# A two-layer hybrid backbone: the order of the feed-forward products, where the modulation is computed, and the last norm's sums

## The chip, the cores and the metric

The kernel runs on one core of a Trainium2 chip. The metric is the device time of one execution in microseconds. Five engines work side by side, each through its own queue in order: TensorE (PE) for matrix products, VectorE (DVE), ScalarE (ACT), GpSimd (POOL), and SyncE (SP), from which this kernel issues its DMAs. An instruction at the head of a queue that waits holds up everything behind it on that engine.

## The reference

Two layers over 1024 latent and 256 context tokens of width 1024, in fp32. Layer 0 mixes tokens by latent attention and windowed attention side by side, layer 1 by differential attention. What the change touches is the modulation, the feed-forward part and the norms:

```python
def layer_norm(x, g, b):
    mu = jnp.mean(xf, -1, keepdims=True)
    var = jnp.mean(jnp.square(xf - mu), -1, keepdims=True)
    return ((xf - mu) * lax.rsqrt(var + LN_EPS) * g + b).astype(x.dtype)

def conv_ffn(h, w_gate, w_up, conv_w, conv_b, w_down):
    g = h @ w_gate
    gp = jnp.pad(g, ((0, 0), (1, 1), (0, 0)))
    g = gp[:, :-2] * conv_w[0] + gp[:, 1:-1] * conv_w[1] + gp[:, 2:] * conv_w[2] + conv_b
    return (jax.nn.silu(g) * (h @ w_up)) @ w_down

def modulation(cond, w_mod, b_mod):
    return jnp.split(jax.nn.silu(cond) @ w_mod + b_mod, 6, axis=-1)

for i in range(DEPTH):
    sh1_l, sc1_l, gt1_l, sh2_l, sc2_l, gt2_l = modulation(c, w_mod[i], b_mod[i])
    ...
    xl = layer_norm(ALPHA * xl + gt1_l * o_l, ln1_g[i], ln1_b[i])
    h_l = xl * (1.0 + sc2_l) + sh2_l
    f_l = conv_ffn(h_l, ffn_w_gate[i], ffn_w_up[i], ffn_conv_w[i], ffn_conv_b[i], ffn_w_down[i])
    xl = layer_norm(ALPHA * xl + gt2_l * f_l, ln2_g[i], ln2_b[i])
```

The hidden width is 2816. Context tokens take the same path in layer 0 with the second conditioning vector `c_ctx`; in layer 1 only the first two of the six modulation vectors are needed for them.

## The kernel before

Activations lie with features on the 128 partitions and tokens along the free dimension. Tokens come in three tiles: 0 and 1 (512 latent tokens each) and 2 (256 context tokens). Every large product is done in a split form: an operand is written as a high part (`hi`, a copy on ACT) and a remainder (`lo`, a subtraction, on DVE or on POOL), and three matmuls stand for one product (`mm`, line 90). A 128 by 512 block of weights is split by `split`; its subtraction is line 87, the copy line 84.

**Seven products for eight.** In the feed-forward part both the up half (gate and up weights at once) and the down half treat their operands as two by two blocks, and use seven products P1 to P7 in place of eight, with sums and differences of blocks formed on DVE. `UP` and `DOWN` give the order of the seven. There are 22 blocks `f` of 128 hidden features. In the up half (`run_up`) one product is 12 matmuls of 512 columns. A first pass computes P1 and P2 for blocks 0 to 11 and writes the results to DRAM (`pre_d`), because these need token tile 0 alone, while the norm of tile 1 is still running. The second pass then does the other five products of blocks 0 to 11 (`EARLY` = 12), one after another, and after that all seven products of blocks 12 to 21. After its last product a block is finished (`finish`: convolution along tokens, silu, product with the up half; lines 1395 to 1399), and stored to DRAM as hidden block `f` two products into the next block. Beside this, `down_sums` forms sums of the down weights for hidden blocks `j` and `j + 11` and writes them to DRAM; it is called in blocks 0 to 10.

In the down half (`run_down`) each of P1 to P7 runs over 11 steps `j`; a step is 12 matmuls into four PSUM banks. Its hidden operand comes from `hidden_operand` (lines 1304 to 1324): P5 writes `b12 - b11` to a temporary tile (three buffers), P6 and P4 change hidden blocks in place. The results of a product are added to the residual by instructions that wait in a list, `late`, and are issued one per group of three matmuls in the next product. When P4 is done, token tile 0 is complete and its norm begins; when P3 is done, tile 1.

**Order of the work.** `advance` prepares operands ahead: six steps in the up half, three in the down half, and issues weight loads two further. Which subtractions go to POOL is written in `prepare`: up P2, P7, P4; down P5, P6, P4. A tile framework places instructions into the engine queues by order of issue and a model of when they are ready, so an instruction of a later step can be placed earlier where its operands and buffers allow it.

**Norms** are generators (`norm`, line 330) that sit in the list `behind`; `tick` advances the first one after every third matmul, and `settle` runs them to the end. A norm adds the eight feature blocks on DVE (line 356), takes their mean over partitions by a product with a constant matrix (line 362), subtracts it (line 351, or 349 on POOL), squares on ACT, adds the squares on DVE (line 373), sums them over partitions by small products (line 380), takes the inverse root, spreads it over partitions by one more product (line 287) and multiplies (line 351). Before each of its PE steps it lets `lag` = 3 ticks pass.

**Modulation of layer 1** (`mod_vectors`, line 163) is advanced beside the second pass of layer 0's up half, 72 advances over its length. For each of twelve halves of 512 values it loads eight 128 by 512 blocks of `w_mod` (two buffers, `opt`), multiplies each by the conditioning value of its partition and accumulates on DVE (lines 185, 187), for shift and scale (chunks 0 and 1) once for each of the two conditioning vectors; then it sums over partitions by four small products for each vector (line 197). The generator is emptied (`drain`) after the up half.

## Time and profile before

| | us |
|---|---|
| median of three runs | 3517.93 |
| lowest and highest | 3513.55, 3519.29 |
| profiled execution, own time | 3515.21 |
| its span | 3513.4 |
| PE / DVE / ACT / POOL busy | 3205.5 / 2650.5 / 1674.3 / 1097.7 |
| layer 0: first pass of the up half | 904.8 to 992.6 |
| second pass: five-product blocks, seven-product blocks | 992.6 to 1234.7, 1234.7 to 1435.1 |
| down half, context part | 1435.1 to 1686.3, 1686.3 to 1907.7 |
| layer 1: first pass | 2790.7 to 2869.3 |
| second pass: five-product blocks, seven-product blocks | 2869.3 to 3053.0, 3053.0 to 3249.0 |
| down half, tail after the last matmul of it | 3249.0 to 3480.2, 3480.2 to 3513.4 |

The span is the time from the first to the last instruction of one profiled execution. Lines such as L87 are lines of the kernel before. A busy PE counts overlapping matmuls, so the number of matmuls in a stretch tells more than its busy time. In a group of instructions, `out<-in` are the program's names of tiles, buffer numbers left out; behind the bar stand the busy time, the mean of one in ns, and the engine's idle time before them with what ended it. The granted clock of PE is 1.00 at full speed.

### The profile page before, as it was taken

The numbers are of one execution on the slowest core, as the hardware profiler recorded it, in microseconds if no ns is written. First come the engines' busy times: TensorE is split into PE (matmuls) and PEld (weight loads), VectorE is DVE, ScalarE is ACT, GpSimd is POOL, SyncE is SP. The second block draws the span as 40 slices with busy tenths as digits, with TensorE's granted clock in tenths as the row PEclk, the third lists the DMA queues.
The fourth block names the chain that finished last, engine by engine and source line by source line (L and its number), as shares of the span: only waits on it lengthen the run. The fifth ranks groups of instructions, "written<-read, shape, count | busy, mean of one in ns | idle before, by whom it ended". The sixth has DMA issues, their size and how long they took to land. (4 is left out here: it accounts for less than half of the span.)

```text
span 3513.4 us, 48532 instructions
## 1 busy us (share of the span) xinstructions
PE 3205.5 (91%) x16772; PEld 2632.9 (75%) x16772; DVE 2650.5 (75%) x4518; ACT 1674.3 (48%) x3161; POOL 1097.7 (31%) x848
## 2 busy tenths in 40 slices
PE   8998999999887899899799999998899999999996
PEld 4466778888666688678698887887778777788775
DVE  3137878875889989677888467778898789976677
ACT  3125778862532233334565345556677443333433
POOL 4245333421311121042543234344522222221132
PEclk9999999999888899999899999999999999999998
DMA  7666233222487744724465665547654468623622
GB/s 227 196 206 195 84 83 85 74 81 83 171 265 240 249 147 146 265 81 129 156 186 156 197 170 157 146 140 210 174 173 142 157 203 271 218 90 109 230 87 87
DMA packets 288007, 568.11 MB, mean 162 GB/s; under 512 B 24785, under 2 KB 111249, under 8 KB 285713
## 3 DMA queue, kind: packets, MB, share of 16 engines
q1 hardware_dynamic: 287760, 565.01, 51.2%
q8 instruction: 132, 2.16, 0.3%
q14 instruction: 115, 0.93, 0.1%
HBM read 419.35 MB, written 145.56 MB: 161 GB/s over the span
## 5 line engine op out<-in xcount | busy, mean ns | idle before, releaser
L87 POOL TENSOR_TENSOR al<-raw,ah 128x512 fp32r<-128x512 f32 x196 | 296.9, 1516 | 665.6 <-ACT ah L84 652.2
L84 ACT ACTIVATE ah<-raw 128x512 fp32r<-128x512 f32 x418 | 260.5, 630 | 434.3 <-PE f L90 294.8
L90 PE MATMUL s<-k,q 128*128 128x512 f32 (+2 forms) x1152 | 307.7, 389 | 15.8 <-ACT sxc L1877 6.8
L87 DVE TENSOR_TENSOR ptl<-tp,pth 128x512 fp32r<-128x512 f32 x412 | 279.6, 684 | 42.2 <-ACT pth L546 37.2
L546 ACT ACTIVATE pth<-tp 128x512 fp32r<-128x512 f32 x412 | 242.3, 595 | 104.9 <-PE tp L542 97.3
L84 ACT ACTIVATE ah<-sum 128x512 fp32r<-128x512 f32 x198 | 122.0, 629 | 342.9 <-DVE sum L1257 172.6
L542 PE MATMUL tp<-ident,p 128*128 128x128 f32 x1648 | 257.6, 276 | 20.7 <-DVE ptl L87 10.2
L90 PE MATMUL f<-al,ah 128*128 128x512 f32 x616 | 245.5, 398 | 10.5 <-DVE al L87 10.3
L90 PE MATMUL f<-ah,al 128*128 128x512 f32 x616 | 243.3, 395 | 7.5 <-POOL al L87 7.5
L90 PE MATMUL f<-ah,ah 128*128 128x512 f32 x616 | 241.3, 395 | 3.0 <-ACT ah L84 3.0
L542 PEld LDWEIGHTS tp<-ident,p 128*128 128x128 f32 x1648 | 197.6, 142 | 52.6 <-DVE ptl L87 10.1
L90 PE MATMUL o<-pth,v 128*128 128x256 f32 x976 | 232.7, 300 | 4.6 <-ACT pth L546 4.5
L87 DVE TENSOR_TENSOR al<-raw,ah 128x512 fp32r<-128x512 f32 x222 | 173.7, 795 | 77.9 <-ACT ah L84 77.8
L90 PEld LDWEIGHTS s<-k,q 128*128 128x128 f32 (+1 forms) x1152 | 189.9, 193 | 45.7 <-ACT p L1890 10.8
L87 POOL TENSOR_TENSOR al<-sum,ah 128x512 fp32r<-128x512 f32 x44 | 67.8, 1541 | 426.0 <-ACT ah L84 384.3
L90 PE MATMUL o<-ptl,v 128*128 128x256 f32 x656 | 185.8, 295 | 16.3 <-DVE ptl L87 15.6
L90 PEld LDWEIGHTS o<-pth,v 128*128 128x128 f32 x976 | 171.2, 192 | 24.2 <-ACT pth L546 7.9
L1887 DVE TENSOR_REDUCE stat<-s 128x1 f32<-128x1024 f32 x128 | 155.6, 1216 | 39.5 <-PE s L90 39.3
L1890 ACT ACTIVATE p<-s,stat 128x1024 f32<-128x1024 f32 x128 | 142.7, 1115 | 82.9 <-DVE stat L1888 67.6
L90 PE MATMUL f<-T,ah 128*128 128x512 f32 x528 | 168.7, 401 | 1.2 <-ACT ah L84 1.2
L90 PE MATMUL f<-b0h,ah 128*128 128x512 f32 x352 | 143.8, 409 | 14.4 <-ACT ah L84 8.8
L87 POOL TENSOR_TENSOR wl<-wraw,wh 128x1024 fp32r<-128x1024 f32 x36 | 91.2, 2533 | 202.7 <-ACT wh L84 200.8
(450 smaller groups left out, 9714.2 us busy)
## 6 DMA issues: line engine op xcount, KB each, us to landing
raw<-w_gate SPq DMA_DIRECT2D x90, 512.0 KB, 4.1
raw<-w_up SPq DMA_DIRECT2D x66, 512.0 KB, 4.3
raw<-w_down SPq DMA_DIRECT2D x66, 512.0 KB, 4.9
wm<-w_mod SPq DMA_DIRECT2D x96, 256.0 KB, 4.2
opt<-w_mod SPq DMA_DIRECT2D x96, 256.0 KB, 3.0
sd<-affy SPq DMA_DIRECT2D x88, 256.0 KB, 4.4
hid<-acc SPq DMA_DIRECT2D x44, 512.0 KB, 3.3
raw<-sd SPq DMA_DIRECT2D x88, 256.0 KB, 2.6
```

The source lines that it names most:

```text
L84: return self.nc.scalar.activation(out, src, AF.Copy)
L87: (eng or self.nc.gpsimd).tensor_tensor(out, src, hi.bitcast(F32), op=ALU.subtract)
L90: self.nc.tensor.matmul(out, lhsT, rhs, start=start, stop=stop)
L542: nc.tensor.transpose(ps[:, n * P : (n + 1) * P], pt[:, kc : kc + P], N.ident[:, :])
L546: nc.scalar.activation(h[:, : n * P], ps[:, : n * P], AF.Copy)
L1887: nc.vector.tensor_reduce(st[:, 2, b, m : m + 1], s[:, :], axis=AX.X, op=ALU.max)
L1890: nc.scalar.activation(p[:, :SEQ], s[:, :], AF.Exp, bias=mx, scale=scale, accum_out=sums[:, b, m, 0:1])
```

## The change

- The second pass of the up half takes blocks in the order 0, 1, 12, 2, 13, 3, ..., 21, 11, so that after two blocks of five products a block of seven and one of five alternate. `rank` is a block's place in this order. `down_sums` is called in every block of odd rank. The loads of hidden blocks for the down half, which were issued as the last block released its operands, start for P1 and P2 in block 21 and for the others in block 11.
- In the second pass P3's subtraction goes to POOL too.
- Chunks 0 and 1 of layer 1's modulation are computed in layer 0's up half by `mod_products`: for each loaded block, four fp32 products on PE with two columns, both conditioning vectors at once, accumulated in PSUM. Forty advances take the place of 72. Chunks 2, 3 and 4 are computed as before on DVE, in layer 0's down half (three advances in four steps, emptied after P4), chunk 5 in layer 1's up half.
- The down half runs P1, P2, P6, P7, P4, P5, P3. P5's operand is formed in place from what P6 left. POOL's subtractions are those of P6, P4, P5 and P3.
- `lag` is 6.
- The last norm (layer 1, tile 1; `alone`) adds the eight blocks by eight products with the constant matrix, adds the squares by small products in PSUM block by block, and lets POOL do two of the eight last multiplies.
- Before the up half the first weights are prepared ahead of the rest of the context tile's norm.

```diff
-        self.lag = 3
+        self.lag = 6
...
+    def mod_products(self, l, chunks, wpool, ppool, ptag):
...
+        for which, half in chunks:
+            ps = self.t(ppool, [P, 512], tag=ptag)
+            for k in range(KT):
+                w = ws.pop(0)
+                for j in range(4):
+                    nc.tensor.matmul(ps[:, 2 * j : 2 * j + 2], w[:, j * P : (j + 1) * P], self.siluc[:, k, 0:2],
+                                     start=k + j == 0, stop=k + j == KT + 2)
+                if todo:
+                    fetch()
+                if k % 2:
+                    yield
+            at = slice(8 * which + 4 * half, 8 * which + 4 * half + 4)
+            b = self.vecs[:, V_BMOD + 48 * l : V_BMOD + 48 * l + 48][:, at]
+            o = self.modv[l][:, at, :]
+            nc.vector.tensor_tensor(o, ps[:, :8].rearrange("p (j c) -> p j c", c=2), b.unsqueeze(2).broadcast_to([P, 4, 2]), op=ALU.add)
+            nc.vector.tensor_scalar(self.sc1[l][:, at, :], o, 1.0, None, op0=ALU.add)
+            yield
...
+        if alone:
+            mean = psum()
+            for i, k in enumerate((4, 5, 6, 7, 0, 1, 2, 3)):
+                nc.tensor.matmul(mean[:, :w], self.mean[:, :], x[k], start=i == 0, stop=i == KT - 1)
...
+                for b in range(nb if alone else 0):
+                    nc.tensor.matmul(st[:, b : b + 1], sq[k - 1][:, b * P : (b + 1) * P], self.mean[:, 0:1],
+                                     start=k == 1 and b == 0, stop=k == KT and b == nb - 1)
...
+        c = copy(bc) if alone else None
         for k in range(KT + 2):
             if k < KT:
-                each(k, bc, None, ALU.mult)
+                each(k, bc, c, ALU.mult)
...
-    DOWN = ("P1", "P2", "P5", "P6", "P7", "P4", "P3")
+    DOWN = ("P1", "P2", "P6", "P7", "P4", "P5", "P3")
...
-        early = [(f, p) for f in range(self.EARLY) for p in self.UP if p not in ("P1", "P2")]
-        rest = [(f, p) for f in range(self.EARLY, NF) for p in self.UP]
+        early, late = range(self.EARLY), range(self.EARLY, NF)
+        blocks = [*early[: -len(late)], *itertools.chain(*zip(late, early[-len(late) :]))]
+        rest = [(f, p) for f in blocks for p in self.UP if f in late or p not in ("P1", "P2")]
+        self.rank = {f: i for i, f in enumerate(blocks)}
...
-            a = self.split(self.raws.pop(n), None if p in ("P5", "P6", "P4") else self.N.nc.vector)
+            a = self.split(self.raws.pop(n), None if p in ("P6", "P4", "P5", "P3") else self.N.nc.vector)
...
-        self.parts[n] = self.split(src, None if p in ("P2", "P7", "P4") and n >= self.n_first else self.N.nc.vector)
+        self.parts[n] = self.split(src, None if p in ("P2", "P7", "P4", "P3") and n >= self.n_first else self.N.nc.vector)
...
-        if p == "P5":
-            return self.add(b12, b11, ALU.subtract)
...
-        put(b21, b21, b11, op=ALU.subtract)
-        return b21
+        if p == "P4":
+            put(b21, b21, b11, op=ALU.subtract)
+            return b21
+        put(b12, b22, b11, op=ALU.subtract)
+        return b12
...
-        for t in (0, 2) if l == 0 else (0,):
-            N.settle(t)
+        N.settle(0)
         N.op.update({p: [y[:, 4 * i : 4 * i + 4, :] for y in N.h[0]] for i, p in enumerate(("P1", "P2"))})
+        self.advance(0)
+        N.settle(2)
...
+            while gone < 40 * (n - self.n_first) // span:
+                next(mods, None)
+                gone += 1
+            if p == "P6" and at % 2:
+                self.down_sums(at // 2)
+            if p == "P7" and at:
+                store(self.blocks[at - 1])
+            if f == end or p in ("P1", "P2") and f == NF - 1:
                 self.leave(p)
...
-    def run_down(self, ready):
+    def run_down(self, ready, mods):
...
+            if n % 4:
+                next(mods, None)
             if j == final and p in ("P4", "P3"):
                 while late:
                     late.popleft()()
+                drain(mods)
                 ready(0 if p == "P4" else 1)
...
+    if l == 0:
+        mods = N.mod_products(1, halves((0, 1)), N.ls, N.qq, "f")
+        more = N.mod_vectors(1, [(*x, (0,)) for x in halves((2, 3, 4))], N.ls, N.qq, "f")
+    else:
+        mods = N.mod_vectors(1, [(*x, (0,)) for x in halves((5,))], N.ls, N.qq, "f")
+        more = iter(())
...
-        N.behind.append((t, N.norm(t, 0, 512, LN_EPS, stages(t))))
+        N.behind.append((t, N.norm(t, 0, 512, LN_EPS, stages(t), alone=t == 1)))
```

More of the change, by code (lines that the diff above doesn't have):

```diff
@@ L203, in mod_vectors, with fetch @@
             yield
+    def mod_products(self, l, chunks, wpool, ppool, ptag):
+        nc = self.nc
+        todo = [(k, 1024 * which + 512 * half) for which, half in chunks for k in range(KT)]
+        ws = []
+        def fetch():
+            k, c0 = todo.pop(0)
+            ws.append(self.t(wpool, [P, 512], tag="opt", bufs=2))
+            self.load(ws[-1][:, :], self.ins["w_mod"][l, k * P : (k + 1) * P, c0 : c0 + 512])
+        fetch()
+        fetch()
+        yield
[7 more added lines that the diff above has]
+                if todo:
+                    fetch()
+                if k % 2:
[5 more added lines that the diff above has]
+            nc.vector.tensor_scalar(self.sc1[l][:, at, :], o, 1.0, None, op0=ALU.add)
+            yield
     def mod(self, l, which, c):
@@ L327, in parts, with norm @@
         return [self.t(pool, [P, KT, TT[t][1]], F32R, tag=f"b{t}{x}") for x in "hl"]
-    def norm(self, t, c0, w, eps, out, sums="sum"):
+    def norm(self, t, c0, w, eps, out, sums="sum", alone=False):
         nc, tmp, pp = self.nc, self.ls, self.qq
@@ L353, in norm @@
         yield
-        acc = total(0)
-        for k in range(1, KT):
-            nc.vector.tensor_tensor(acc, x[0] if k == 1 else acc, x[k], op=ALU.add)
-            if k % 2:
+        nb = w // P
+        if alone:
[3 more added lines that the diff above has]
+        else:
+            acc = total(0)
+            for k in range(1, KT):
+                nc.vector.tensor_tensor(acc, x[0] if k == 1 else acc, x[k], op=ALU.add)
+                if k % 2:
+                    yield
+            for _ in range(self.lag):
                 yield
-        for _ in range(self.lag):
-            yield
-        mean = psum()
-        nc.tensor.matmul(mean[:, :w], self.mean[:, :], acc, start=True, stop=True)
+            mean = psum()
+            nc.tensor.matmul(mean[:, :w], self.mean[:, :], acc, start=True, stop=True)
         yield
@@ L365, in norm @@
         acc, sq = total(1), {}
+        if alone:
+            st = psum()
         for k in range(KT + 2):
@@ L1421, in run_up @@
             evacuate(n, f, p, ps[:, :])
-            if n >= self.n_first:
-                while gone < 72 * (n - self.n_first) // span:
-                    next(mods, None)
-                    gone += 1
-                if p == "P6" and f < NF // 2:
-                    self.down_sums(f)
-                if p == "P7" and f:
-                    store(f - 1)
-                if p == "P3":
-                    if f + 1 < self.EARLY:
-                        again(f + 1)
-                    if f == NF - 1:
-                        self.leave(p)
-                    finish(f)
-            if f == NF - 1 and p != "P3":
-                self.leave(p)
-        self.last = lambda: (store(NF - 1), self.load_hidden(1, (NF // 2 - 1,)), self.load_residual(1))
+            if n < self.n_first:
+                continue
+            at = self.rank[f]
+            while gone < 40 * (n - self.n_first) // span:
[6 more added lines that the diff above has]
+            if f == end or p in ("P1", "P2") and f == NF - 1:
+                self.leave(p)
+            if p == "P3":
+                if f != end and self.blocks[at + 1] < self.EARLY:
+                    again(self.blocks[at + 1])
+                finish(f)
+        self.last = lambda: (store(end), self.load_hidden(1, (0,)), self.load_residual(1))
     def leave(self, p):
```

40 lines of the change are left out of this document (21 added, 19 removed).

## The prediction

> **What bounds the kernel now.** I read the page first, then stage windows, then who made TensorE (PE) wait in each stage, then the groups on VectorE (DVE), then the chain that ended last.
>
> ```profile
> PE 3205.5 (91%) x16772; PEld 2632.9 (75%) x16772; DVE 2650.5 (75%) x4518; ACT 1674.3 (48%) x3161; POOL 1097.7 (31%) x848
> DVE  3137878875889989677888467778898789976677
> ```
>
> PE is the bound overall, but DVE stands at 9 tenths where the feed-forward halves run. The windows cut these halves at their first and last products. Columns: window and length, then busy us and instructions of PE, PEld, DVE, ACT, POOL, granted clock, DMA share, GB/s.
>
> ```profile
> 992.60:1234.70 242.10, 198.69 (x793) 160.49 (x792) 226.75 (x325) 61.16 (x83) 37.94 (x24) 0.85 0.75 246
> 1234.70:1435.10 200.40, 200.40 (x889) 163.42 (x887) 174.66 (x253) 71.38 (x100) 36.67 (x28) 1.00 0.50 158
> 1435.10:1452.90 17.80, 2.01 (x10) 1.71 (x9) 7.16 (x8) 2.93 (x3) 0.00 (x0) 0.66 1.04 403
> 1452.90:1686.30 233.40, 219.59 (x937) 177.78 (x937) 170.82 (x237) 102.90 (x177) 70.98 (x46) 0.97 0.41 130
> ...
> 2869.30:3053.00 183.70, 174.05 (x721) 137.88 (x720) 172.17 (x223) 58.75 (x80) 46.33 (x23) 0.97 0.79 264
> 3053.00:3249.00 196.00, 196.00 (x841) 157.68 (x840) 146.08 (x193) 72.49 (x104) 40.03 (x29) 1.00 0.29 98
> 3249.00:3280.50 31.50, 28.22 (x123) 22.38 (x121) 18.85 (x28) 12.71 (x21) 0.00 (x0) 1.00 1.01 392
> 3280.50:3480.20 199.70, 190.80 (x815) 152.19 (x815) 154.95 (x207) 84.55 (x148) 56.86 (x40) 0.99 0.35 107
> 3480.20:3513.40 33.20, 6.00 (x13) 2.78 (x12) 19.60 (x32) 8.64 (x13) 6.61 (x7) 0.58 0.17 63
> ```
>
> Rows 1 to 4 are layer 0: five-product blocks, seven-product blocks, the turn from up to down, the down half. Rows 5 to 8 are the same in layer 1, row 9 the tail. In the seven-product rows PE never idles: 70 products of 12 matmuls, 840, take 196.0 us, so 0.2333 us each and 2.80 us a product. Sixty products at that rate are 168.0 us, yet the five-product rows took 242.1 and 183.7. There DVE is nearly always busy: in layer 1 172.17 / 12 = 14.3 us a block, against 14.0 us of PE; in the seven-product row 146.08 / 10 = 14.6 against 19.6. One kind starves PE, the other leaves DVE idle. In layer 0 DVE also carries the modulation of layer 1. Waits of PE in the first row, then in rows 3 and 4 together:
>
> ```profile
> PE f L197 <- DVE sum L187: 39.1, 5, 12.2
> PE f L90 <- ACT ah L84: 3.7, 1, 3.7
> ```
>
> ```profile
> PE f L197 <- DVE sum L187: 15.8, 1, 15.8
> PE f L90 <- POOL al L87: 7.5, 1, 7.5
> ```
>
> L197 is the column sum of a finished modulation accumulator. It stands in PE's queue among products whose operands may be ready; when DVE is behind, the products behind it wait too. The 15.8 is the drain of the generator at the turn of the halves.
>
> **The change, part by part.** *Order of blocks and the modulation, layer 0 up.* After blocks 0 and 1, seven and five products alternate. A pair holds 33.6 us of PE and 14.3 + 14.6 = 28.9 us of DVE, less two P3 subtractions that go to GpSimd (POOL), at the mean of this group of row 5:
>
> ```profile
> L87 DVE TENSOR_TENSOR al<-sum,ah 128x512 fp32r<-128x512 f32 x34 | 26.4, 775 | 0.0
> ```
>
> That is 27.4 of 33.6, 82%, while row 2 ran without a PE wait at 174.66 / 200.4 = 87%. So the second pass should be PE's: 130 x 12 x 0.2333 = 364.0. Chunks 0 and 1, for both conditioning vectors, leave DVE (64 accumulations; 0.75 each by the row below, 48 us) and become 4 halves x 8 x 4 = 128 small fp32 products on PE. Nearest rows: four column sums of the norm, also 128x128 fp32 weights against one column, eight records, once in running work and once after a pause (both in the chain below): 0.80 and 1.88 us. In running work 0.20 a product: 128 x 0.20 = 25.6. The 32 column sums that go (6.4) are inside the 242.1 and 200.4. Sum 389.6. For stalls I add 4 (none in row 2, 15.7 in row 5, the nearer case being row 2). Old 442.5, new 393.6: **-48.9** (from -52.9 at no stall to -33 at 20).
>
> *Layer 1 up.* Chunk 5 comes here: 16 accumulations on DVE (12 us over the first third, 41 products, 115 us) and 8 column sums, 1.6. 364.0 + 1.6 + 3 = 368.6 against 183.7 + 196.0 = 379.7: **-11.1** (-14.1 to -4).
>
> *The turn and the down half.* 77 steps x 12 x 0.2333 = 215.6; the norm of tile 0 in between costs PE two wide fp32 products and four column sums, 0.95 + 0.80 + 0.95 by the chain, 2.7. The first half's hidden blocks are now fetched when P2 of block 21 ends, ten products before the down half and not five; the residual and the last loads stay where they were, so DMA (1.04 and 1.01 of its share at the turn) has 14 us more. No drain is left at layer 0's turn, since 21 of the 40 advances empty the generator halfway. In the down half P6 now rewrites the hidden blocks in place directly after P2; P5, which needed a temporary of three buffers, comes after P4 and reuses b12. So P6's subtractions can run ahead during P1 and P2. Those that ran during P5 cost this (GpSimd's timeline, layer 0):
>
> ```profile
> 1526.07 13.68 POOL L87 TENSOR_TENSOR al<-raw,ah 128x512 fp32r<-128x512 f32 x3 [3.16 <-ACT ah L84]
> 1542.35 1.29 POOL L87 TENSOR_TENSOR al<-raw,ah 128x512 fp32r<-128x512 f32 x1 [2.60 <-ACT ah L84]
> ```
>
> Three subtractions took 13.68 that one does in 1.29 afterwards, while DVE worked without a pause; behind it is the 7.5 us wait above. The Trainium skill ("SBUF — State Buffer", section "Who interferes with whom") says that a DVE instruction with two SBUF inputs and a GpSimd instruction that reads SBUF exclude one another, and the one already running holds the other off whole. The row agrees. It speaks against this change, which gives GpSimd 22 more subtractions in each up half and 11 in each down half; by it one more such run in each layer would add 2 x 7.5 = 15, to 3439.
>
> Layer 0's down half also takes chunks 2 to 4: 48 accumulations and 24 column sums (4.8 of PE):
>
> ```profile
> L187 DVE SCALAR_TENSOR_TENSOR sum<-opt,siluc,sum x112: 734/746/1782, 1011.5 to 1450.4; 128x512 f32<-128x512 f32 x112
> ```
>
> 48 x 0.75 = 36 us more on a DVE that is 170.82 of 233.4 busy: about 89%, near row 2's 87%. I therefore leave 12 us of stalls in layer 0 (bounds 0 and the old 35) and 4 in layer 1 (bounds 0 and the old 13). Layer 0: 251.2 to 215.6 + 4.8 + 2.7 + 12 = 235.1, **-16.1** (-28 to -2). Layer 1: 231.2 to 215.6 + 2.7 + 4 = 222.3, **-8.9** (-13 to -3).
>
> *Last norm.* From the chain: start, length, what.
>
> ```profile
> 3449.48 0.95 PE f L362 x2
> ...
> 3462.00 0.80 PE f L380 x8
> ...
> 3481.58 0.61 DVE sum L356
> ...
> 3485.86 2.09 PE f L362 x2
> ...
> 3487.97 0.61 ACT bcs L344
> ...
> 3488.60 3.68 DVE acc L351 x6
> 3492.28 0.61 DVE sum L373
> ...
> 3496.97 0.70 DVE sum L373
> ...
> 3497.71 1.88 PE f L380 x8
> ...
> 3501.74 2.06 PE f L287 x2
> ...
> 3503.83 0.69 DVE acc L351
> ...
> 3508.74 0.81 ACT acc L1627
> ```
>
> Mean: eight wide products on a warm PE, 8 x 0.95 = 7.6, from 3480.2 to 3487.8; now 3487.95, so nothing. Squares: they follow the subtractions on ScalarE (ACT) at 0.63, each with four column sums behind it (0.80): first square 3489.9, then eight times 0.80: 3496.3 instead of 3499.6, -3.3. Spread: 0.95 on a warm PE, not 2.06, -1.1. Last multiply: DVE does six of eight, but GpSimd now has two multiplies beside its four scalings:
>
> ```profile
> 3488.65 2.51 POOL L349 TENSOR_TENSOR acc<-acc,bcs 128x512 f32<-128x512 f32 x2 [16.60 <-ACT bcs L344]
> ...
> 3504.62 0.77 POOL L1629 TENSOR_SCALAR acc<-acc,vecs 128x512 f32<-128x512 f32 x1 [3.75 <-DVE acc L351]
> ```
>
> 2.51 + 4 x 0.77 = 5.6 after the first multiply (0.69), 6.3 in all against 5.7 now, +0.6. Tail **-3.8**. If PE goes slow in its gaps of about 2 us, the squares alone pay 8 x (1.88 - 0.80) = 8.6 more: bounds -6 and +6. The Trainium skill ("TensorE: Matmul & The Clock Gate", section "What's actually happening") halves the clock after an idle window of some 3.4 us; by that the warm price stands and the tail is as summed, by the other 3433.
>
> *Lag 6.* Each norm's PE work comes three ticks (nine matmuls, 2.1 us of wide ones) later, where PE had waited for DVE's adds; in the windows 893 to 993, 1690 to 1740 and 2734 to 3060:
>
> ```profile
> PE f L380 <- DVE sum L373: 2.7, 1, 2.7
> ```
>
> ```profile
> PE f L380 <- DVE sum L373: 8.9, 1, 8.9
> ```
>
> ```profile
> PE f L380 <- DVE sum L373: 4.7, 2, 4.6
> ```
>
> It can give about 2.1 + 1 (short matmuls in the context stage) + 2.1. Against it: nine more ticks, 6.3 us, leave more of layer 0's context norm to the flush before the up half; that is partly answered by preparing the first weights ahead of it. I take **-3** (-8 to +6). That tile 0's last norm now has 88 ticks, not 44, to hide in costs nothing beyond what stands above.
>
> Sum: -48.9 - 11.1 - 16.1 - 8.9 - 3.8 - 3.0 = -91.8. The profiled execution took 3515.21 (span 3513.4): 3423.4. The median 3517.93 is 2.7 higher: **3426**.
>
> **Rivals.** *The wait moves with the accumulations.* In layer 0's down half PE meets six groups of column sums with DVE 89% full. At 39.1 / 5 = 7.8 us each that is 47, 35 more than I left: 3461. For it: the same in-order wait in both fences; against: none in row 2 at 87%.
>
> *Alternating does not even DVE out*, because its queue is in order and the bursts of a five-product block reach past the six prepared steps: each layer keeps row 5's 15.7 us, 12.7 + 11.7 more: 3450. Against: the first sixty us of row 5, in which PE never idles.
>
> ```profile
> 2869.30:2930.00 60.70, 60.70 (x263) 49.23 (x262) 53.85 (x72) 19.60 (x27) 14.56 (x8) 1.00 0.81 270
> ```
>
> *Every floor is reached:* -52.9 - 14.1 - 28 - 13 - 6 - 8 = -122, 3396.
>
> *Slower: PE waits for the modulation's weights.* The small products read `opt` straight from DMA, two buffers, and a buffer is fetched again only after PE has read it. Pairs come every 130 / 40 = 3.25 products, 9.1 us, sixteen of them.
>
> ```profile
> DMA to landing us min/median/max: 2.5/3.0/12.2
> ```
>
> A load that takes x leaves PE x - 9.1 us idle, and what follows runs at 1.88, not 0.80: 32 x 1.08 = 34.6. The gain is gone when 16(x - 9.1) + 34.6 = 91.8, at x = 12.7; at 14, 3539. Against: that is above the longest landing of the row, whose median is 3.0; for: a load issued behind a blocked store on SP's queue counts the block too.
>
> **How the numbers follow.** Forecast 0.58; moved wait 0.14; all floors 0.13; no evening out 0.09; slower 0.04; two of the milder ones together, ending about where it was, 0.02. Range 3394 to 3464: from the floors to just past the moved wait. Faster by over 0.2% (7 us, about what can be told from no change) is the first four, 0.94; within 0.02; slower 0.04.
>
> **What would show it.** Second passes of about 394 and 369 us, PE never waiting for DVE at a column sum there, and DVE nowhere at 9 tenths for long. The 256 records of the small products at about 0.10 us. No PE gap at layer 0's turn, and no GpSimd subtraction of over 5 us in the down halves. A tail of 29 us. I am wrong on the main step if either second pass is over 405 or 380, wrong on the moved work if PE waits over 12 us at column sums in the down half, and wrong on the slower side's price if PE waits for `opt` at all.

## The result, and the profile after

The changed kernel takes 3438.23 us (median of four runs, 3431.79 to 3442.20) against 3516.88 for the kernel before in the same comparison (3513.55 to 3519.29): a ratio of 0.9775, 95% interval 0.9758 to 0.9793. The prediction said 3426, range 3394 to 3464: the sign and size are right, and the sum came out 12 us too low. The profiled execution took 3431.79, with a span of 3429.8.

The page of the changed kernel, engines and the strip of VectorE (DVE):

```profile
PE 3214.0 (94%) x17034; PEld 2652.3 (77%) x17034; DVE 2589.0 (75%) x4364; ACT 1670.0 (49%) x3162; POOL 1190.2 (35%) x916
...
DVE  3137878884887798887887377778898789997784
```

TensorE (PE) is busy for 8.5 us more in a span that is 83.6 shorter. DVE still shows 8 and 9 tenths in the layer 1 up half; three slices in a row stand at 9, which the prediction's sign "DVE nowhere at 9 tenths for long" had excluded. It is not idle more often, it is only no longer late. The windows, cut at the first matmul of each stage as before (layer 0: second pass of up, down half; layer 1: the same; tail):

```profile
978.50:1369.70 391.20, 391.20 (x1818) 322.56 (x1817) 316.12 (x412) 134.25 (x187) 115.21 (x75) 1.00 0.62 202
1369.70:1621.80 252.10, 230.74 (x985) 186.91 (x984) 210.46 (x296) 106.17 (x182) 80.18 (x59) 0.95 0.59 194
2796.60:3161.10 364.50, 364.50 (x1578) 295.62 (x1576) 332.67 (x411) 128.55 (x186) 125.29 (x76) 1.00 0.60 200
3161.10:3396.90 235.80, 223.70 (x950) 179.28 (x948) 173.44 (x231) 97.81 (x168) 67.99 (x51) 0.98 0.42 141
3396.90:3429.80 32.90, 16.77 (x70) 13.80 (x70) 8.83 (x15) 9.02 (x14) 9.02 (x9) 0.58 0.17 64
```

In both second passes PE is busy for the whole window: not one wait. In the down halves it is not, and the tail is as long as it was. Term by term, in us, against the prediction:

| Stage | Before | After | Change | Predicted |
|---|---|---|---|---|
| layer 0, second pass of up | 442.5 | 391.2 | -51.3 | -48.9 |
| layer 1, second pass of up | 379.7 | 364.5 | -15.2 | -11.1 |
| layer 0, turn and down half | 251.2 | 252.1 | +0.9 | -16.1 |
| layer 1, down half | 231.2 | 235.8 | +4.6 | -8.9 |
| tail | 33.2 | 32.9 | -0.3 | -3.8 |
| everything else ("lag 6") | 2175.6 | 2153.3 | -22.3 | -3.0 |
| span | 3513.4 | 3429.8 | -83.6 | -91.8 |

The up halves did what was forecast and a little more; the 25 us that the down halves were to give did not come; the 22 us of the last line but one were not foreseen. Two errors of some 20 to 30 us cancel in part; that the total came so close is to that extent luck.

PE's waits in layer 0's down half, after:

```profile
PE f L90 <- DVE al L87: 13.3, 7, 4.1
PE f L90 <- ACT ah L84: 3.7, 1, 3.7
PE f L424 <- DVE sum L417: 3.2, 1, 3.2
PE f L197 <- DVE sum L187: 0.7, 1, 0.7
```

The waits are for operands (al, ah), and hardly for the modulation's column sums (L197, 0.7). To see where they lie I cut each down half at the first matmul of each of its seven products. A product without any wait takes 29.9 us for its 132 matmuls (three of them in layer 1 do); the table gives what each took beyond that, waits, small products and matmuls at a lower clock together.

| Kernel, layer | P1 | P2 | P6 | P7 | P4 | P5 | P3 |
|---|---|---|---|---|---|---|---|
| before, layer 0 | 2.4 | 0 | 2.2 | 0 | 0 | 11.0 | 3.8 |
| after, layer 0 | 9.2 | 1.9 | 6.3 | 1.1 | 7.9 | 9.2 | 7.3 |
| before, layer 1 | 5.7 | 0 | 2.6 | 0 | 0 | 7.5 | 5.8 |
| after, layer 1 | 9.8 | 1.7 | 0 | 0 | 0 | 9.3 | 5.2 |

(Before, P5 stood third. Layer 0 before has 17.8 us of turn ahead of P1 and 4.7 between P3 and the context stage; after has neither.) In layer 1 the stall of 10.1 at the change from P2 to P5 and P6 is gone, as forecast. What took its place: P1 +4.1, P2 +1.7, the product beside which tile 0's norm lies +3.5 (P3 before, P5 after), and 5.2 new in P3. In layer 0 P6 and P4 have stalls that layer 1 has not.

The chain that ended last, the tail of the changed kernel (start, length, what):

```profile
3394.08 1.72 PE f L391 x4
...
3396.87 2.00 PE f L391 x4
3398.87 0.02 issue
3398.89 0.61 ACT bcs L377
...
3400.25 0.64 ACT affy L412
3400.89 0.04 issue
3400.93 12.75 PE f L414 x64
...
3415.73 2.09 PE f L319 x2
...
3418.59 2.50 POOL acc L382 x2
```

L391 is the mean, eight wide products in 16 records; the first 12 of these already run inside P3 (that is P3's 5.2). L414 is the column sums of the squares: 64 records in 12.75 us, 0.20 each, where 0.10 had been taken.

### The profile page after: what moved, and what is told of

It reads as the page before. It is cut to its first block, busy times and chain, and to the rows that moved or that the text cites. A ratio compares the mean times of both kernels' runs of the same rounds, so it can differ in the third digit from the quotient of the medians.

```text
span 3429.8 us, 48960 instructions
## 1 busy us (share of the span) xinstructions
PE 3214.0 (94%) x17034; PEld 2652.3 (77%) x17034; DVE 2589.0 (75%) x4364; ACT 1670.0 (49%) x3162; POOL 1190.2 (35%) x916
## 4 chain that ended last, share of the span: by engine, by line
PE 65%; DVE 13%; issue 6%; POOL 6%; DMA 5%; ACT 5%; SPq 0%; POOLq 0%; ACTq 0%; DVEq 0%
PE f L90 40%; PE s L90 6%; PE tp L90 4%; PE o L90 4%; PE tp L587 3%; PE acc L90 3%; DVE ptl L87 2%; DVE al L87 1%; PE mod L145 1%; POOL wl L87 1%; PE f L224 1%; DVE stat L1075 1%; DVE p L1960 1%; DVE stat L1946 1%; ACT pth L591 1%
## 5 line engine op out<-in xcount | busy, mean ns | idle before, releaser
L87 POOL TENSOR_TENSOR al<-raw,ah 128x512 fp32r<-128x512 f32 x218 | 324.2, 1488 | 660.7 <-ACT ah L84 537.6
L587 PEld LDWEIGHTS tp<-ident,p 128*128 128x128 f32 x1648 | 198.6, 143 | 51.9 <-DVE ptl L87 10.1
L87 POOL TENSOR_TENSOR al<-sum,ah 128x512 fp32r<-128x512 f32 x88 | 134.0, 1523 | 289.3 <-ACT ah L84 269.4
L84 ACT ACTIVATE ah<-sum 128x512 fp32r<-128x512 f32 x176 | 106.7, 625 | 156.3 <-PE f L90 130.0
L87 DVE TENSOR_TENSOR al<-raw,ah 128x512 fp32r<-128x512 f32 x200 | 156.0, 792 | 21.8 <-ACT ah L84 21.5
L90 PEld LDWEIGHTS f<-al,ah 128*128 128x128 f32 x616 | 118.7, 193 | 48.9 <-DVE al L87 23.2
```

What stands on the lines that cost most here:

```text
L84: return self.nc.scalar.activation(out, src, AF.Copy)
L87: (eng or self.nc.gpsimd).tensor_tensor(out, src, hi.bitcast(F32), op=ALU.subtract)
L90: self.nc.tensor.matmul(out, lhsT, rhs, start=start, stop=stop)
L587: nc.tensor.transpose(ps[:, n * P : (n + 1) * P], pt[:, kc : kc + P], N.ident[:, :])
```

## The experiments

The theory at this point: alternation and the moved modulation carry the up halves; in the down halves the accumulations (layer 0), the last group of weight sums (now at the turn) and the norms cost what the new order gave; the tail's sums run at half clock. Each run changes one thing against the changed kernel unless said; times are medians, stage times are from the profiled execution. The changed kernel's own runs span 10 us, and the attention stages that none of these edits touches took between 1097 and 1108 us, so totals within some 8 us say little. Beside each group of runs the kernel before was timed again, with medians from 3512.70 to 3516.88. Stage times mostly repeat to about 1 us; the largest differences of a stage that the edit leaves alone are 5.3 us (layer 1's pass in the second experiment) and 3.6 (layer 0's down half in the sixth).

**All modulation on DVE, in layer 0's up half.**

```
-        mods = N.mod_products(1, halves((0, 1)), ...)
-        more = N.mod_vectors(1, [... halves((2, 3, 4))], ...)
+        mods = N.mod_vectors(1, [(*x, (0, 1) if x[0] < 2 else (0,)) for x in halves(range(6))], ...)
+        more = iter(())
...
+        mods = more = iter(())
...
-            while gone < 40 * (n - self.n_first) // span:
+            while gone < 80 * (n - self.n_first) // span:
```

> All twelve half chunks of layer 1's modulation are accumulated on VectorE inside layer 0's second pass of up; none on TensorE, none in the down halves or in layer 1. Rest as in the changed kernel. Theory (VectorE's load is what the move of the modulation relieves): 128 accumulations of 0.746 us are 95.5 us on top of the 316.1 us that VectorE is busy in that pass, so 412 us, more than the 364.0 + 16 x 0.80 = 376.8 us of TensorE: the pass becomes VectorE's, 410 to 425 us against 391.2; layer 0's down half, 252.1 with 36 us of accumulations, falls to 236 to 242; total up by 5 to 20. Rival (alternation alone brings the gain, the place of the modulation does not matter): pass at 377 to 382, total down by 10 or more.

3469.79 us, +32. Second pass 441.9, down half 238.3. The pass and the total are longer than expected: DVE's load became PE's time, 34.0 of the 50.7 us as waits at the column sums (the granted clock is 0.90 and 0.95 in the two halves of the pass, so the matmuls take longer too). The PE waits in the pass:

```profile
PE f L197 <- DVE sum L187: 34.0, 9, 6.3
PE f L90 <- ACT ah L84: 2.1, 1, 2.1
```

This is the wait of the kernel before (39.1, five times) again, in alternating blocks. In the down half P6, P7 and P4 take 0, 0 and 0 beyond 29.9 (6.3, 1.1 and 7.9 with the accumulations); P1, P5 and P3 stay at 10.8, 9.2, 7.2. So the accumulations, with their column sums, cost 15 us in layer 0's down half, and P5's stall is not theirs.

**The rest of the modulation in the up half.** Chunks 0 and 1 stay on PE.

```
+        mods = itertools.chain(N.mod_products(1, halves((0, 1)), ...),
+                               N.mod_vectors(1, [... halves((2, 3, 4))], ...))
+        more = iter(())
-            while gone < 40 * ...
+            while gone < 66 * ...
```

> Chunks 0 and 1 stay on TensorE, but the accumulations of chunks 2 to 4 move from layer 0's down half into its second pass of up. Theory (the 48 accumulations are what stalls layer 0's down half): the pass takes 391.2 + 24 x 0.20 = 396 us with VectorE at (316.1 + 36) / 396 = 89%, no wait of TensorE; the down half falls from 252.1 by 4.8 of column sums and some 8 to 12 of stalls to 236 to 240; total down by 7 to 12, 0.2 to 0.35%. Rival (the down half waits for its own operands, the accumulations only lie in the gaps): down half 246 or more, total within 3 us. Rival 2 (89% is too much for the pass): pass over 402.

3452.62 us, +14, where a fall was expected. Second pass 408.6, down half 245.4: rival 2. P6, P7 and P4 lose nothing, but P1 loses 17.9; why it does is not settled. The waits of PE in the pass:

```profile
PE f L90 <- DVE al L87: 4.3, 4, 1.6
PE f L224 <- DMA opt<-w_mod: 2.1, 1, 2.1
PE f L197 <- DVE sum L187: 0.5, 1, 0.5
```

They are 6.9 of the 17.4 us that the pass grew by; 4.8 are the column sums, and the rest I cannot place. The accumulations cost about as much in the up half as in the down half; of these two places neither is free. The wait for `opt`, the mechanism of the prediction's slower side, shows here once with 2.1 us; in the changed kernel it does not show.

**The old order of blocks**, with the loads at the turn in that order too; the P3 subtraction stays on GpSimd (POOL), the modulation stays spread.

```
-        blocks = [*early[: -len(late)], *itertools.chain(*zip(late, early[-len(late) :]))]
+        blocks = [*early, *late]
-            if p == "P6" and at % 2:
-                self.down_sums(at // 2)
+            if p == "P6" and at < NF // 2:
+                self.down_sums(at)
...
```

> Blocks in the order 0 to 21 again (all five-product blocks, then all seven-product ones), with the loads at the turn in that order too; everything else of the change stays, so the P3 subtraction is on GpSimd and the modulation is spread. Theory (alternation carries layer 1's gain): layer 1's pass takes 375 to 380 us, as before the change (379.7), not 364.5, and its first twelve blocks show the waits again; layer 0's pass gains most of what it gained, since the modulation stays off VectorE: 400 to 408 against 391.2. Total up by 20 to 28. Rival (the P3 subtraction on GpSimd carries it: 12 x 0.775 = 9.3 us off VectorE's 172.2 in the five-product blocks): layer 1's pass 365 to 369, total within 5 us of the changed kernel.

3479.68 us, +41, against 20 to 28 expected. Layer 1's pass is 391.8, longer than the 375 to 380 expected; layer 0's is 403.2, as expected. The windows of layer 1, five-product blocks and seven-product blocks:

```profile
2811.00:3006.80 195.80, 179.38 (x734) 139.24 (x733) 184.70 (x237) 59.77 (x82) 58.28 (x37) 0.97 0.81 271
3006.80:3202.80 196.00, 196.00 (x845) 158.94 (x844) 147.51 (x178) 72.44 (x104) 54.77 (x39) 1.00 0.29 100
```

Alternation carries layer 1's gain: 27.3 us of pass between the two orders, more than the 15.2 gained against the kernel before. The rival is out: with P3's subtraction on GpSimd and the old order, the five-product row takes 195.8 us, 12.1 more than before (183.7). What has come to it is chunk 5: its 16 accumulations (12 us) fall in the first third, where DVE is busy for 184.70 of 195.8 us. That they cost the 12 us is argued, since this row also holds the moved subtraction and no run parts the two; with alternation the pass has no wait with both in it. In layer 0 alternation is worth 12.0, so most of that pass's gain is the modulation's, as the first experiment also says.

**The old order of products in the down half.**

```
-    DOWN = ("P1", "P2", "P6", "P7", "P4", "P5", "P3")
+    DOWN = ("P1", "P2", "P5", "P6", "P7", "P4", "P3")
```

with P5's temporary and the old division of subtractions.

> The down half runs its products in the old order P1 P2 P5 P6 P7 P4 P3, with P5's operand in the three-buffer temporary and the old set of subtractions on GpSimd in the down halves. Theory (the new order moved the stall, it removed little: 5 to 9 us less at the change from P2 to P6, and 4 to 7 us more at the turn and in P5, where the norm of tile 0 now falls): layer 0's down half 248 to 258 against 252.1, layer 1's 231 to 238 against 235.8, total within 5 us of the changed kernel. Rival (the new order gains what the prediction gave it, and something else took it back): both down halves longer by 8 or more each, total up by 15 or more.

3443.41 us, +5. Layer 0's down half 244.7 (-7.5), layer 1's 240.2 (+4.5): the first lies below its expected range (248 to 258), the second above (231 to 238). The total comes out about as expected all the same, because one term lies elsewhere: the first 351 matmuls of the context stage, right behind layer 0's P3. Windows of this run, then of the changed kernel, then of the kernel before:

```profile
1611.70:1694.50 82.80, 55.69 (x364) 52.18 (x363) 71.85 (x121) 47.82 (x86) 44.90 (x36) 0.77 0.44 144
```

```profile
1621.80:1694.80 73.00, 54.18 (x365) 49.84 (x365) 65.36 (x107) 40.16 (x74) 36.44 (x28) 0.81 0.41 133
```

```profile
1686.30:1760.50 74.20, 54.26 (x363) 51.67 (x364) 65.17 (x111) 41.95 (x77) 38.52 (x31) 0.79 0.51 167
```

With lag 6 and only the 44 ticks of P3, tile 0's norm is not done when P3 ends, and the context stage pays 9.8 us. With lag 3 (before) it paid 1.2, behind the gap of 4.7 named above. So the new order and lag 6 belong together: with lag 6 the earlier completion of tile 0 is worth 10 us here, and costs part of it inside P5 and P3. In layer 1 of this run P3 loses 10.3, of which the mean's products are 5.2; the norm beside it thus costs 5.1, with lag 6 too.

**Lag 3.**

```
-        self.lag = 6
+        self.lag = 3
```

> The norms' lag is 3 again, not 6. Theory (the lag gave only little, the preparing ahead gave more): the stages before layer 0's up half lengthen by 2 to 6 us in all, total up by 2 to 6. Rival (the lag is what took 14.1 us out of layer 0's first stage and 7.0 out of layer 1's): total up by 15 or more. Rival 2 (the extra ticks cost in the flush ahead of the up half): total down by 3 or more.

3446.29 us, +8, more than expected. The stage ahead of the second pass of layer 0 (the first pass; windows of this run, the changed kernel, and the kernel before):

```profile
895.90:985.20 89.30, 77.97 (x300) 60.63 (x301) 74.75 (x118) 53.09 (x94) 28.98 (x22) 0.88 0.61 205
```

```profile
898.20:978.50 80.30, 74.50 (x303) 58.67 (x302) 73.73 (x118) 52.06 (x92) 26.45 (x22) 0.95 0.63 215
```

```profile
904.80:992.60 87.80, 77.51 (x301) 60.38 (x302) 71.00 (x108) 47.32 (x82) 19.25 (x13) 0.88 0.61 203
```

The lag is worth 9.0 us in this one stage, against 3 that I had for it in all, and 1.5 at the start of the context stage; it costs 3.6 in layer 0's P3 (7.3 with lag 6, 3.7 here), where the column sums of tile 0's norm now fall. The granted clock rises from 0.88 to 0.95 with it: with lag 3 PE waits for the norm's sum (L424), in the changed kernel it does not.

```profile
PE f L424 <- DVE sum L417: 3.6, 1, 3.6
```

**No weights prepared ahead of the context's settling.**

```
         N.settle(0)
-        self.advance(0)
         N.settle(2)
```

> The first weight steps of the up half are no longer prepared between the settling of tile 0 and of the context; they are prepared after both, as before the change. Theory (preparing ahead gave most of the 14.1 us at layer 0's start and little at layer 1's, where no context norm is settled): layer 0's stage up to the second pass lengthens by 6 to 12, total up by 6 to 12. Rival (it is the lag): total within 3 us.

3441.08 us, +3, and the same stage takes 80.3, as with it. The rival: it is the lag. Preparing ahead gives nothing that can be seen.

**The last norm as before the change.**

```
-        N.behind.append((t, N.norm(..., alone=t == 1)))
+        N.behind.append((t, N.norm(..., alone=False)))
```

> The last norm is computed as before the change: adds of its blocks and of their squares on VectorE, then one mean product and four column sums; the last multiply is divided as before. All else as in the changed kernel. Theory (the column sums at half clock, 12.7 us for 64 records where 6.4 was priced, ate the gain): the tail after the last product takes 32 to 35 us against 32.9, total within 3 us. Rival (the sums on TensorE gain the 3.8 priced, and another effect, such as the mean's products standing in P3, hides it): tail 35 to 37, P3 shorter by 3, total within 2 us again but by two changes that show apart in the windows.

3425.91 us, ratio to the kernel before 0.9747 (0.9730 to 0.9763), 12 us below the changed kernel in the median; the two intervals touch at their ends, so that it is the faster is likely and not settled by the totals. P3 of layer 1 loses 0 instead of 5.2, and the tail is 33.2, no longer than with the sums on PE. Its chain, mean and column sums:

```profile
3391.39 0.60 DVE sum L395
...
3396.93 2.09 PE f L401 x2
...
3408.78 1.88 PE f L424 x8
...
3412.71 2.09 PE f L319 x2
```

Its mean, after seven adds, begins 5.6 us after the last product (3391.3), and from the mean's end to the end of the column sums it is 11.6 us (3399.02 to 3410.66) where the changed kernel takes 14.8 (3398.87 to 3413.68). From the end of the spreading product (L319) to the end of the span it is 9.6 us here and 12.0 in the changed kernel, whose chain runs over the two multiplies given to GpSimd. The changed kernel's earlier mean is eaten by these two. By the stages, the part of the change that moved the last norm's sums to PE costs 5 us; the medians differ by 12, the rest being within the spread of the runs.

**The weight sums in ranks 1 to 11.**

```
-            if p == "P6" and at % 2:
-                self.down_sums(at // 2)
+            if p == "P6" and 1 <= at <= NF // 2:
+                self.down_sums(at - 1)
```

> The sums of the down weights are formed behind the blocks of rank 1 to 11 and not of rank 1, 3, ... 21, so none is left for the last block ahead of the turn. Theory (the last group of sums, 1 MB read and 1 MB written with four VectorE adds, crowds the turn, whose DMA share is 0.90): P1 of the down half loses 4 us, not 8 to 9, in each layer; total down by 6 to 10. Rival (the turn waits for the last block's own chain: conv, silu, store, hidden block, split): P1 unchanged, total within 3 us. Rival 2 (eleven groups of sums in half the time crowd VectorE and SP's queue): second passes longer by 3 or more each, total up.

3450.98 us, +13. The theory for P1 and rival 2 both hold: P1 loses 5.9 and 4.7, not 9.2 and 9.8, so the last group of sums does cost 3 to 5 us at each turn; and the second passes grow to 398.2 and 381.7, with PE waiting in layer 1's:

```profile
PE f L90 <- DVE al L87: 11.1, 4, 5.2
```

**Sums in even ranks, P5 ahead of P4, the last norm's blocks 4 to 7 added first.**

```
-    DOWN = ("P1", "P2", "P6", "P7", "P4", "P5", "P3")
+    DOWN = ("P1", "P2", "P6", "P7", "P5", "P4", "P3")
-            if p == "P6" and at % 2:
+            if p == "P6" and (at == 1 or at and at % 2 == 0):
-        N.behind.append((t, N.norm(..., alone=t == 1)))
+        N.behind.append((t, N.norm(..., alone=False, last=t == 1)))
```

> Four edits that fall into different stages. The sums of the down weights go behind the blocks of rank 1, 2, 4, ... 20 (seven-product ones) and not of odd rank (five-product ones, the last block among them). P5 runs ahead of P4, not after it, so the norm of tile 0 falls beside P3, whose operand needs no subtraction, and no longer beside P5, whose operand needs one. The last norm is on VectorE's adds again, but adds the blocks 4 to 7, which are complete before P3 ends, ahead of 0 to 3. Theory, against the changed kernel: second passes unchanged (391 and 364.5, within 2); P1 of the down half loses 4 to 5 us in each layer, not 8 to 9, since no 2 MB of sums stand at the turn; the product beside the norm loses 4 to 5 us, not 8.4; P3 of layer 1 no longer carries the mean's products (-5); tail 30 to 31.5 against 32.9. Down halves 243 to 246 and 221 to 224 against 252.2 and 235.6; total 3405 to 3415. Rival (the turn waits for the last block's own chain, and the norm costs 8 us wherever it lies): down halves 250 and 229, total 3422 to 3428.

3470.82 us, +33: a clear miss. Only the tail (31.2) is as expected. Layer 1's pass is 381.8: P6 of nearly every even rank from 8 on starts 1 to 2 us late. P1 loses 19.2 and 18.6. Layer 1's turn, first on DVE, then a wait of ScalarE (ACT), SyncE's (SP's) queue and PE (start, length, what, and the idle time before it; for the wait, us in total, times, longest):

```profile
3202.88 0.69 DVE L1306 TENSOR_TENSOR affy<-raw 128x512 f32<-128x512 f32 x1 [7.71 <-DMA sd<-affy]
...
3206.69 1.28 DVE L1447 SCALAR_TENSOR_TENSOR acc<-acc,vecs 128x1023 f32<-128x1023 f32 x1 [2.52 <-ACT acc L1446]
3207.89 0.68 DVE L1420 TENSOR_TENSOR u<-f,u 128x512 f32<-128x512 f32 x1
```

```profile
ACT acc L1446 <- DMA hid<-acc: 10.8, 1, 10.8
```

```profile
3197.09 0.32 SPq L77 DMA_DIRECT2D hid<-acc  x1
```

```profile
3208.63 0.80 PE L90 MATMUL f<-ah,ah 128*128 128x512 f32 x1 [5.85 <-DVE u L1420]
```

PE needs a bank that DVE has to empty (L1420) and stands 5.85 us. Two waits lie ahead of L1420 in DVE's queue. An add of the weight sums (L1306) stands 7.71 us for a buffer whose store is under way, but that wait ends at 3202.88, as PE's begins (3202.78). What ends last is the other: DVE stands 2.52 us for the convolution's first step on ACT (L1446), and that stands 10.8 us for the store of a hidden block, issued at 3197.09. On SP's queue that store comes right behind stores of the weight sums; whether these made it late no run separates. So denser sums stall the passes, sums that end early relieve the turn, and the odd ranks of the change are the best of the three placings tried; why P1 loses twice as much here, although the last group is called five products earlier than in the change, is only in part explained. Moving P5 ahead of P4 gains nothing in layer 1 (9.3 moves from P5 to P3: with GpSimd doing the subtractions of both, the norm costs 9.3 beside either), and the context stage pays 9.9 again, as with the old order.

**The squares summed by wide products**, on the kernel of the last experiment: eight products with the matrix of 1/1024, the power taken over 128x512.

```
+                if last:
+                    nc.tensor.matmul(st[:, :w], self.mean[:, :], sq[k - 1], start=k == 1, stop=k == KT)
...
+            nc.gpsimd.tensor_tensor(bc[:, :w], bc[:, :w], self.neghalf[:, 0:1].broadcast_to([P, w]), op=ALU.pow)
```

> As i_even_p5_order, but in the last norm each block's squares are summed over the partitions by one wide product with the matrix of 1/1024 (eight products of 2 records each, accumulated), which leaves the variance in every partition; the power -0.5 is taken over 128x512 on GpSimd, and the diagonal and the spreading product fall away. Theory (TensorE's clock falls to half in the tail because the one-column products hardly use it, not because it stands idle): during the eight wide products, which follow each other at 0.92 to 0.95 us, the granted clock stays at 0.9 or more, and they end 8 to 9 us after the first square, not 12.75. Rival (the clock falls in any case some 8 us after the last bf16-like product): the products take 2.0 us each and 16 us in all. What the wide power costs is not known from a row: 1.02 us is the row for 128x4; between 1 and 10 us. Tail 26 to 38.

3551.26 us, for one row:

```profile
L429 POOL TENSOR_TENSOR bcs<-bcs,neghalf 128x512 f32<-128x512 f32 x1 | 81.9, 81927 | 9.5 <-DVE bcs L428 9.5
L415 PE MATMUL f<-affy,mean 128*128 128x512 f32 x16 | 9.8, 782 | 2.1 <-ACT affy L413 2.1
```

The power costs 81.9 us. The question asked is answered all the same: the wide products take 9.8 us. Windows over them (the second holds the later ones), and below it the changed kernel's windows over its one-column products; the granted clock is the third figure from the end:

```profile
3440.00:3448.00 8.00, 6.25 (x9) 2.67 (x10) 3.68 (x6) 3.95 (x7) 2.51 (x2) 0.55 0.00 0
3448.00:3452.00 4.00, 3.55 (x9) 1.29 (x7) 0.34 (x1) 1.26 (x2) 0.00 (x0) 1.00 0.00 0
```

```profile
3400.90:3405.00 4.10, 4.07 (x25) 4.07 (x25) 2.30 (x4) 2.35 (x4) 1.18 (x1) 0.65 0.00 0
3405.00:3413.70 8.70, 8.67 (x41) 8.58 (x41) 0.00 (x0) 1.89 (x3) 0.00 (x0) 0.50 0.00 0
```

After the same 2.07 us of idleness the wide products bring the clock back to 1.00; among the one-column products it falls to 0.50 and stays there, though PE is busy without a gap. My expectation that it stays at 0.9 throughout did not hold: it was down at first and came back. The rival, 16 us for the products, did not hold either.

**The modulation of layer 0's down half spread wider**, on the same kernel.

```
-            if n % 4:
+            if n % 5 < 3:
```

> As i_even_p5_order, but layer 0's down half goes on with the modulation in 3 of 5 steps and not in 3 of 4, so the 48 accumulations lie over 62 steps and not over 49. Theory (VectorE's load in P6 and P4 or P5 is the cause of the stalls there): layer 0's down half is 2 to 5 us shorter than in i_even_p5_order. Rival (bursts of a single step, not the mean load, make the stalls): within 2 us, the stalls only lie elsewhere. Layer 1 unchanged.

3462.27 us. Layer 0's down half 247.6 against 255.2: P6 loses 1.6 and P5 4.9, where it was 6.0 and 8.0; 1.2 of the 7.6 are P1, and P4 takes 1.9 back. The rate matters, as expected, beyond the size expected.

**The three edits that helped, together.** The changed kernel's order and sums, the last norm on DVE with blocks 4 to 7 first, the modulation in 2 of 3 steps.

```
-            if n % 4:
+            if n % 3:
-        N.behind.append((t, N.norm(..., alone=t == 1)))
+        N.behind.append((t, N.norm(..., alone=False, last=t == 1)))
```

> The changed kernel with three edits that the runs so far point to: the last norm on VectorE's adds again, blocks 4 to 7 added first; and the modulation in layer 0's down half in 2 of 3 steps, not 3 of 4, so that its 37 pieces end just as P4 does. Order of products, place of the sums of the down weights, lag 6 as in the changed kernel. Theory: layer 1's down half 230 to 231 (no mean products in P3) against 235.6, tail 31 against 33.0, layer 0's down half 246 to 252 against 252.2 by stalls in P6 and P4 of 5.4 and 7.0 that shrink, second passes and the context stage unchanged; total 3418 to 3428, ratio to the kernel before 0.972 to 0.975. Rival (thinner accumulations only push a stall on into P4, as the generator then ends there): layer 0's down half 251 or more and total 3424 to 3432.

3422.36 us (3420.34 to 3430.61), ratio 0.9735 (0.9719 to 0.9750): faster than the changed kernel (0.9758 to 0.9793), and not told apart from the experiment with the old last norm alone (0.9730 to 0.9763). Its windows of layer 0's down half, layer 1's down half and the tail:

```profile
1366.30:1615.60 249.30, 230.41 (x985) 185.22 (x984) 208.86 (x296) 106.29 (x182) 82.31 (x59) 0.96 0.59 197
...
3163.20:3392.90 229.70, 217.94 (x937) 176.95 (x935) 176.28 (x234) 97.72 (x168) 68.77 (x51) 0.98 0.43 144
3392.90:3423.60 30.70, 5.73 (x13) 2.58 (x12) 17.42 (x29) 8.64 (x13) 6.58 (x7) 0.56 0.19 68
```

The thinner accumulations take 4.1 us out of P6 (2.2) and 3.2 out of P4 (4.7), and P5 takes 4.6 back (13.8): in that the rival holds too.

## Why the prediction was right, and where it was not

*Second passes, right.* Layer 0: 364.0 for the products, and 16 groups of 16 small records at 1.70 us, 27.2, are 391.2, which is the window. The price of 0.10 a record held (25.6 predicted), the 4 us of stalls were not there. The row of the small products, durations min, median, max in ns (their ends overlap, so the spacing was read from the groups):

```profile
L224 PE MATMUL f<-siluc,opt x256: 166/251/251, 1000.8 to 1191.0; 128*128 128x2 f32 x128
```

Layer 1: 364.0 predicted for the products, 364.5 measured with all stalls and sums. That alternation evens DVE out is shown for layer 1 by the old block order. The argument by DVE's share (82%, since 87% had run without a wait) came out right and is no limit: layer 1's pass runs without a wait at 332.67 / 364.5 = 91%.

*Down halves, wrong.* The step that failed is "I therefore leave 12 us of stalls in layer 0 and 4 in layer 1". Beyond 7 x 29.9 = 209.3 the prediction's sums leave 25.8 and 13.0 for sums, norm and stalls; the table's rows add up to 42.9 and 26.0. (The rate of 0.2333 us a matmul was read in the up half; in the down half it is 29.9 / 132 = 0.2265, so 6.3 us of each predicted sum were room that the prediction did not know of.) Four terms, by the experiments:
- *Accumulations, layer 0.* 15 us, gone when they lie elsewhere; the prediction had counted 4.8 of column sums apart. "About 89%, near row 2's 87%" was the reading that failed. The stalls lie in P6 and P4, whose operands DVE also forms in place, and thinner accumulations shrink them; that it is these steps' own demand that makes the difference is argued, not shown.
- *The turn.* The prediction held that DMA has 14 us more there. It costed the earlier loads and overlooked that `down_sums` goes from the blocks 0 to 10 to every odd rank, the last block among them: 1 MB read, 1 MB written and four adds. Without them P1 loses 3.3 and 5.1 less; 5 to 6 remain.
- *Tile 0's norm.* "Costs nothing beyond what stands above" was wrong. Beside P5 it costs 9.3, where it cost 5.8 beside P3 before. Lag 6 is not the reason, since in the old order it costs 5.1 with lag 6; and P5 ahead of P4 does not help (9.3 beside P3). The likeliest difference left is the new division of subtractions, under which GpSimd does those of P5 and P3; no run tries it alone. In layer 0 the norm also spreads into P3. That with lag 6 the old order would lose 10 us at the context stage was not foreseen either.
- *The mean's products.* They run in P3 for 5.2 us. They were costed at "nothing", from 3480.2 on, as if they began only after the last product. The tail has them back: its mean ends 2.0 us after the last product and not 7.8.

*The stall from P2 to P6, right.* It is gone in layer 1. So is the drain at layer 0's turn. The slow subtractions on GpSimd are gone too; the longest of layer 0's down half:

```profile
L87 POOL TENSOR_TENSOR al<-raw,ah x46: 1263/1296/2390, 1435.8 to 1620.4; 128x512 fp32r<-128x512 f32 x46
```

It is 2.39 us, with 46 of them where there were 33. The estimate of 15 us that I drew from the Trainium skill ("SBUF — State Buffer", "Who interferes with whom") did not come true. That does not speak against the exclusion itself: these rows neither show it nor rule it out. (From the forecast of 3426 its 15 us make 3441, not 3439, and the 8.6 us of a slow clock in the tail 3435, not 3433.)

*Tail, size wrong.* Predicted -3.8, measured -0.3, and that with 5.8 us of the mean moved ahead into P3. By the chains, from the mean's end to the end of the column sums it takes 14.8 us and not 11.6: +3.2, where -3.3 was forecast. The column sums were priced at 0.80 a block and took 12.74 / 8 = 1.6; the prediction had the other bound (squares at 1.88 a block, +6 in all) and chose the wrong end, because PE has no long gap. The spread takes 2.09 where 2.06 was to become 0.95. The last multiply, from the spread's end on, takes 12.0 and not 9.6: +2.4, where +0.6 was forecast.

*Lag 6, size wrong.* -3 was taken. The stage ahead of layer 0's second pass alone went from 87.8 to 80.3, and lag 3 takes 9.0 back there. Of the other 14.8 us of the "everything else" line, 7.1 are the context stage and layer 1's attention, which vary as much between kernels that do not touch them; 1.1 are layer 1's first pass; 6.6 lie ahead of layer 0's up half, where lag 3 takes nothing back (its first product starts at 895.9 us, in the changed kernel at 898.2). What these 6.6 are stays open.

*Rivals.* None of them took place as it was put: the wait at column sums of the down half is 0.7 us, the five-product blocks were evened out, `opt` was never waited for. What took the down halves' gain no rival named: operands late behind DVE's queue, and the mean's products.

## What to carry to other kernels

When one engine starves another in bursts, reorder the work so that heavy and light blocks alternate before moving operations between engines: here that removed every wait at a DVE load of 91%, and the same load in the old order cost 27 us. Count, for each moved step, what it meets in every in-order queue at its new place: the accumulations, the weight sums and the norm all fitted by their busy share and all stalled the products behind them. A pipelining distance and the order of the work around it are one setting: lag 6 gains 9 us in one place, and with the old order of products loses 10 in another.

## What was not expected of the hardware

One-column products neither keep TensorE's clock up nor bring it back. 64 records issued without a gap ran at a mean granted clock of 0.65 in their first 4.1 us and 0.50 in the next 8.7; 16 wide records in the same place, after the same pause, started at 0.50 as well and brought it to 1.00. The fall itself can't be put down to them alone: the clock went down 3.3 us after the last wide product here, and 3.6 us after it with the old last norm, where PE stood idle. In the prediction I drew on the Trainium skill ("TensorE: Matmul & The Clock Gate", "What's actually happening"), by which the clock halves after an idle window of some 3.4 us; I read "idle" as an empty engine. The trace does not agree with that reading: PE was busy for 4.07 of 4.10 us and 8.67 of 8.70. The 256 records of small products in the second pass kept their 0.10 us, between wide ones.

A power on GpSimd gets dear with size: 1.02 us for 128x4, 81.9 us for 128x512, 80 times the time for 128 times the elements.
